# Four places of a hybrid decoder trunk in a new order: gate matmuls, retention scores, the end of the first RWKV half, and transposes of attention probabilities

## The chip, the cores and the metric

The kernel runs on one core of a Trainium2 chip. The metric is the time of one execution on the device in microseconds, lower is better. Three runs of the kernel before gave 884.91, 885.19 and 886.32 us, so its time is the median, 885.19 us.

## The reference

The program computes two decoder layers for 256 tokens of width 1024. Layer 0 mixes tokens with RWKV-7 (8 heads of 64) and with chunkwise retention (8 heads of 64) side by side; layer 1 mixes them with differential attention (8 heads, two softmaxes each). Each layer then attends to 256 memory tokens and runs an MLP of width 4096. The parts that the change touches are these:

```python
def rwkv7_time_mix(pa, mu, w0, w2, a0, a2, g2, k_k, k_a, r_k, ln_w, ln_b):
    ...
    w_log = -jax.nn.softplus(-(w0 + jnp.tanh(wd) @ w2)) - 0.5
    decay = jnp.exp(-jnp.exp(w_log.astype(jnp.float32)))
    a = jax.nn.sigmoid(a0 + ad @ a2)
    g = jax.nn.sigmoid(gd) @ g2
    ...
    y = wkv7_scan(r_h, hd(decay), k_h, v_h, -kk, kk * a_h)
    y = group_norm(y, ln_w, ln_b, A_GN_EPS)
    y = y + jnp.sum(r_h * k_h * r_k, axis=-1, keepdims=True) * v_h
    return y.reshape(bsz, s, A_WIDTH) * g

def retention(pb, ln_w):
    ...
    scores = jnp.einsum('bhncd,bhnmd->bhncm', qc, kc) * dmat[None, :, None]
    inner = jnp.einsum('bhncm,bhnme->bhnce', scores, vc)
    ...

def diff_attention(h, w_in, lq1, lk1, lq2, lk2, ln_w, w_out, rel_bias, lam_init):
    q, k, v = jnp.split(h @ w_in, 3, axis=-1)
    ...
    logits = jnp.einsum('bhcqd,bhckd->bhcqk', q_blk, k).astype(jnp.float32) * scale + bias[None, :, None]
    p = jax.nn.softmax(logits, axis=-1)
    attn = p[:, :, 0] - lam * p[:, :, 1]
    o = jnp.einsum('bhqk,bhke->bhqe', attn.astype(v.dtype), v)
    ...

def reference(x, mem, ...):
    for layer in range(DEPTH):
        ...
        h = h + mix
        h = h + memory_cross_attention(rms_norm(h, norm_cross_w[layer]), mem_n, ...)
        h = h + squared_relu_mlp(rms_norm(h, norm_mlp_w[layer]), mlp_w1[layer], mlp_w2[layer])
    return rms_norm(h, final_norm_w)
```

## The kernel before

**The weight stream.** All large products are f32 products made of three matmuls on rounded parts. A weight piece of 512 KB lands in `raw` (a DMA on SyncE's queue, four buffers). ScalarE writes its rounded high part `hi`, VectorE the rest `lo` (both line 129, three buffers each). TensorE multiplies high by high, low by high and high by low. These matmuls run through the whole program as a stream, piece after piece, 24 matmuls of 256 columns or 12 of 512 a piece. A second kind of matmul is plain f32 on small tiles; it shows in the trace as two records for each instruction.

**PSUM banks.** There are eight: four of the pool `acc`, two of `mm`, two of `tr` (functions `acc_t`, `mm_t`, `tr_t`). Whoever asks a pool for a tile gets its next bank in turn, and the first matmul into it waits until the last reader of that bank is done.

**What sets the order.** The framework's scheduler fixes the order of each engine's instructions when the program is built, by dependencies and by the order in which the code is written; on the chip each engine runs its list in that order.

**The gate stage (lines 425 to 434).** `psw` and `psa` are products of 64 rows each, one in the lower and one in the upper row half of the array (`w2a2[0:64]` and `w2a2[64:128]`), in two batches (`b0` of 0 and 2), with two `tr` banks a batch. ScalarE's sigmoids into `sg` (line 434) and `a` empty them. Then come products with the head pattern for `kk` (two columns each) and transposes of `v` (`tok_major`, line 500).

**Retention scores (lines 632 to 648).** `kTr` and `qTr` hold two heads in each 128 rows. For each `hq` and each row half `h2`, four matmuls fill one `mm` and one `tr` bank; VectorE multiplies by the mask (lines 646, 648) and ScalarE copies the rest (line 647). Beside this VectorE runs the triangular inverse of the RWKV part (lines 591, 593). `ret_T` (line 686) later transposes the retention output `xn`.

**The RWKV halves.** A loop over four groups `g` makes `LV`, `U` and states `S`. `outputs(0)` stands behind group 2, then `finish(0)` and `outputs(1)` behind the loop, then six `kv_chunk`s of memory keys and values. `outputs` ends in a group norm: `sm`, `yc`, `ysq`, `s2`, then `rs` on GpSimd (line 226), then `yc` times `rs` (line 748). `finish` transposes `yc` (line 757), applies weights on ScalarE (`ya`, line 759) and multiplies by the gate.

**Differential attention (lines 1077 to 1186).** For `c` of 0 to 3, `proj_cols` makes two heads of q and two of k from four weight pieces. `heads(hd)` makes a head's logits (`kTd`, `qTd`) and its softmaxes, subtracts them into `z` (line 1125), transposes `z` (line 1128) into a `tr` bank, and ScalarE copies that to `PTd` (line 1129). Heads of pair `c - 1` are written behind the projections of pair `c`. `v_proj` makes the values, `attend` multiplies `PTd` by `Vd`, `to_oT` transposes the result.

Of the kernel before, what the change touches and what calls it, by code (L numbers as in the profile page):

```python
# [8 lines left out]
F32 = mybir.dt.float32  # L9
F32R = mybir.dt.float32r  # L10
AF = mybir.ActivationFunctionType
# [26 lines left out]
def kernel(ctx: ExitStack, tc: tile.TileContext, ins: dict, out: bass.AP):  # L38
# [29 lines left out]
    def nm(s):  # L68
        cnt[0] += 1
        return f"{s}_{cnt[0]}"  # L70

    def acc_t():
        return ps_acc.tile([128, 512], F32, tag="acc", name=nm("acc"))

    def mm_t():
        return ps_mm.tile([128, 512], F32, tag="mm", name=nm("mm"))

    def tr_t():
        return ps_tr.tile([128, 512], F32, tag="tr", name=nm("tr"))
# [39 lines left out]
    def mm(o, lhsT, rhs, start, stop):  # L119

        ins = nc.tensor.matmul(o, lhsT=lhsT, rhs=rhs, start=start, stop=stop)  # L121
        key = o.tensor.name
        prev = last_in_bank.get(key)
        if prev is not None:
            behind(ins, prev, "one accumulation group per bank")
        last_in_bank[key] = ins
# [296 lines left out]
    a_ = t4(prep, "a")  # L423
    nc.scalar.activation(wa_[0:64, :], wa_[0:64, :], AF.Tanh)
    for b0 in (0, 2):
        psw = tr_t().rearrange("p (b t) -> p b t", b=2)
        psa = tr_t().rearrange("p (b t) -> p b t", b=2)
        for j in range(2):
            cs = slice((b0 + j) * 128, (b0 + j + 1) * 128)
            mm(psw[:, j, :], lhsT=w2a2[0:64, cs], rhs=wa_[0:64, :], start=True, stop=True)  # L430
            mm(psa[:, j, :], lhsT=w2a2[64:128, cs], rhs=wa_[64:128, :], start=True, stop=True)
        for j in range(2):
            b = b0 + j
            nc.scalar.activation(sg[:, b, :], psw[:, j, :], AF.Sigmoid, bias=prm[:, R_W0 + b:R_W0 + b + 1])
            nc.scalar.activation(a_[:, b, :], psa[:, j, :], AF.Sigmoid, bias=prm[:, R_A0 + b:R_A0 + b + 1])
# [193 lines left out]

    PT0 = []  # L630
    cmb = cmask.unsqueeze(1).broadcast_to([128, 2, 128])
    for hq in range(2):
        p0 = rp.tile([128, 4, 256], F32, tag=f"qk{hq}", name=nm("PT0"))
        p1 = PT1[hq]
        PT0.append(p0)
        for h2 in range(2):
            pr = slice(h2 * 64, h2 * 64 + 64)
            ps = mm_t().rearrange("p (h c) -> p h c", h=2)
            ps1 = tr_t()[:, :256].rearrange("p (h c) -> p h c", h=2)
            for i in range(2):  # L640
                hp = 2 * hq + i
                mm(ps[:, i, :], lhsT=kTr[pr, hp, 0:128], rhs=qTr[pr, hp, :], start=True, stop=True)
                mm(ps1[:, i, :], lhsT=kTr[pr, hp, 128:256], rhs=qTr[pr, hp, 128:256], start=True, stop=True)
            d0 = p0.rearrange("p (i h) c -> p h i c", i=2)[:, h2]
            d1 = p1.rearrange("p (i h) c -> p h i c", i=2)[:, h2]
            nc.vector.tensor_tensor(d0[:, :, 0:128], ps[:, :, 0:128], cmb, op=ALU.mult)
            nc.scalar.activation(d0[:, :, 128:256], ps[:, :, 128:256], AF.Copy)
            nc.vector.tensor_tensor(d1, ps1, cmb, op=ALU.mult)

    def g_evac(ps, t):  # L650
        nc.scalar.activation(gR[:, t, :], ps, AF.Sigmoid)
# [164 lines left out]
        if g == 2:  # L816
            outputs(0)

    finish(0)
    outputs(1)  # L820


# [1 line left out]
    V0 = xpool.tile([128, 2, D], F32, tag="xAl", name="V0")  # L824
    for i in range(6):
        kv_chunk(0, i, KT0, V0)
    KT1 = [kv1pool.tile([128, 8, 256], F32R, tag="KT1", name="KT1h")]
    V1 = kv1pool.tile([128, 2, D], F32, tag="V1", name="V1")
    kv1_left = [4, 5, 0, 1, 2, 3]
# [247 lines left out]
    def diff(before, after):  # L1077
# [15 lines left out]
        r1 = dp.tile([128, 2, 8], F32, tag="r1", name="r1")  # L1093
        r1q = dp.tile([128, 2, 8], F32, tag="r1q", name="r1q")

        def heads(hd):
            zt = [dp.tile([128, 2, 128 * (t + 1)], F32, tag=f"z{t}", name=nm("z"), bufs=2) for t in range(2)]

            ps = [acc_t() for _ in range(2)]
            for t in range(2):  # L1100
# [10 lines left out]
            for t in range(2):  # L1111
# [11 lines left out]
                cf = small.tile([128, 1], F32, tag="cf", name=nm("cf"))  # L1123
                nc.vector.tensor_scalar(cf, sm[:, 0:1], rc[:, 1:2], nlam, op0=ALU.mult, op1=ALU.mult)
                nc.vector.scalar_tensor_tensor(z3[:, 0, :], z3[:, 1, :], cf, z3[:, 0, :], op0=ALU.mult, op1=ALU.add)
                pt = tr_t()
                for k in range(t + 1):
                    nc.tensor.transpose(pt[:, k * 128:(k + 1) * 128], z3[:, 0, k * 128:(k + 1) * 128], ident)  # L1128
# [2 lines left out]
        for c in range(4):  # L1131
            proj_cols(I["w_dqk"], 2 * c, xT, lambda ps, c=c: nc.scalar.activation(qT[:, 2 * c:2 * c + 2, :], ps, AF.Copy), c == 0)
            proj_cols(I["w_dqk"], 8 + 2 * c, xT, lambda ps, c=c: nc.scalar.activation(kT[:, 2 * c:2 * c + 2, :], ps, AF.Copy))
            if c > 0:
                heads(2 * c - 2)
                heads(2 * c - 1)
        heads(6)
        heads(7)
        nc.vector.tensor_tensor(r1q, r1, r1, op=ALU.mult)
        oT = next_xT()  # L1140
        onorm = {}

# [4 lines left out]
        def attend(hq, t, po):  # L1147
# [8 lines left out]
            nc.scalar.activation(sq, o3, AF.Square)  # L1156
            s2 = small.tile([128, 4], F32, tag="s24", name=nm("s2"))
            nc.vector.tensor_reduce(s2, sq, axis=AX.X, op=ALU.add)
            nc.vector.tensor_tensor(s2, s2, r1q[:, t, 4 * hq:4 * hq + 4], op=ALU.mult)
            rs = rstd_of(s2, 128, 4, EPS)  # L1160
            nc.vector.tensor_tensor(rs, rs, r1[:, t, 4 * hq:4 * hq + 4], op=ALU.mult)
# [9 lines left out]
                         oT[1][:, 4 * hq:4 * hq + 4, t * 128:(t + 1) * 128], ps, wdif)  # L1171

        v_proj(0)
        for t in range(2):
            attend(0, t, acc_t())
        v_proj(1)
        for t in range(2):
            to_oT(0, t)
# [144 lines left out]
```

## Time and profile before

| what | value |
|---|---|
| median of three runs | 885.19 us |
| the profiled execution | 886.23 us |
| span of its trace | 884.5 us |
| TensorE busy | 864.1 us (98%) |
| VectorE busy | 590.8 us (67%) |
| ScalarE busy | 455.3 us (51%) |
| share of TensorE in the chain that ended last | 88% |

The profiled execution is 1.04 us above the median; 1.7 us of it lie outside the span. TensorE is the bound nearly everywhere, so a stage's time is that of TensorE's list plus TensorE's idle time, and the places to look at are its idle gaps, its slow records and the switches out of the stream.

### The profile page before, as it was taken

Reading aid. Unit: us, or ns where it says so; the run is one execution under the profiler, and the core shown is the slowest. Engines: PE = TensorE matmul, PEld = TensorE weight load, DVE = VectorE, ACT = ScalarE, POOL = GpSimd, SP = SyncE. Lnnn points to the kernel's source line nnn. Section 1 sums busy time; section 2 is a strip of 40 time slices with the busy share of each in tenths; the row PEclk is TensorE's granted clock in tenths of the full one; section 3 lists DMA queues with packets and bytes.
Section 4 is the critical chain, followed back from the end, with each engine's and each line's share of the span. In section 5 each row is a group of like instructions: output and inputs, shape, how many; then the busy total and the mean of one; then the engine's idle time right before and its main releaser. Section 6 shows DMA issues by size and latency. Waiting matters only on the chain.

```text
span 884.5 us, 14111 instructions
## 1 busy us (share of the span) xinstructions
PE 864.1 (98%) x5546; PEld 746.8 (84%) x5546; DVE 590.8 (67%) x932; ACT 455.3 (51%) x730; POOL 30.3 (3%) x51
## 2 busy tenths in 40 slices
PE   7999999999999999999999999999999999999996
PEld 5988889878889888888888899878998888888885
DVE  5668898564586576666666666786776776666665
ACT  5765444244475455444444455575654554444443
POOL 2000001010000000000000000001000000000001
PEclk7999999999999999999999999999999999999999
DMA  8654444125664647556566655534552465555561
GB/s 314 233 160 120 118 137 139 50 81 185 189 218 165 207 145 240 190 190 190 188 190 191 187 178 167 143 120 140 180 173 103 148 204 186 192 192 186 193 188 63
DMA packets 47078, 149.98 MB, mean 170 GB/s; under 512 B 4731, under 2 KB 4900, under 8 KB 46884
## 3 DMA queue, kind: packets, MB, share of 16 engines
q1 hardware_dynamic: 45456, 142.73, 50.0%
q10 hardware_dynamic: 1108, 3.72, 1.3%
q0 software_dynamic: 448, 2.63, 1.0%
q8 instruction: 43, 0.70, 0.3%
q14 instruction: 23, 0.19, 0.1%
HBM read 148.01 MB, written 2.63 MB: 170 GB/s over the span
## 4 chain that ended last, share of the span: by engine, by line
PE 88%; DVE 5%; issue 3%; ACT 2%; POOL 1%; DMA 1%; POOLq 0%; SPq 0%; DVEq 0%; ACTq 0%
PE acc L121 36%; PE mm L121 36%; PE tr L121 13%; DVE lo L129 1%; ACT hi L129 1%; PE tr L254 1%; POOL rs L226 1%; DMA h<-in_x_dram 1%; PE tr L1128 1%; PE tr L975 1%; DVE z L1109 0%; PE acc L254 0%; DVE xn L268 0%; PE tr L500 0%; POOL xn L1206 0%
## 5 line engine op out<-in xcount | busy, mean ns | idle before, releaser
L129 DVE TENSOR_TENSOR lo<-raw,hi 128x1024 fp32r<-128x1024 f32 x262 | 320.2, 1224 | 220.2 <-ACT hi L129 218.0
L129 ACT ACTIVATE hi<-raw 128x1024 fp32r<-128x1024 f32 x262 | 277.6, 1060 | 328.5 <-PE mm L121 119.6
L121 PE MATMUL mm<-xhl,hi 128*128 128x256 f32 (+1 forms) x784 | 188.0, 319 | 1.0 <-ACT xhl L129 0.7
L121 PEld LDWEIGHTS mm<-xhl,hi 128*128 128x128 f32 x784 | 129.7, 189 | 11.8 <-ACT xhl L129 1.7
L121 PE MATMUL mm<-xhl,lo 128*128 128x256 f32 x512 | 138.2, 282 | 0.0
L121 PE MATMUL acc<-hi,hl 128*128 128x512 f32 x256 | 100.2, 392 | 0.0
L121 PE MATMUL acc<-hi,hh 128*128 128x512 f32 x256 | 100.2, 391 | 0.0
L121 PE MATMUL acc<-lo,hh 128*128 128x512 f32 x256 | 99.7, 390 | 0.0
L121 PEld LDWEIGHTS mm<-xhl,lo 128*128 128x128 f32 x512 | 96.7, 189 | 2.5
L121 PE MATMUL tr<-xhl,hi 128*128 128x512 f32 x256 | 92.8, 396 | 0.0
L121 PE MATMUL acc<-hi,xhl 128*128 128x512 f32 x256 | 81.9, 396 | 0.0
L121 PE MATMUL tr<-xhl,lo 128*128 128x256 f32 x256 | 66.8, 281 | 0.0
L121 PEld LDWEIGHTS acc<-hi,hl 128*128 128x128 f32 x256 | 48.1, 188 | 11.2 <-DVE hl L129 0.9
L121 PEld LDWEIGHTS acc<-lo,hh 128*128 128x128 f32 x256 | 48.1, 188 | 10.4
L121 PEld LDWEIGHTS acc<-hi,xhl 128*128 128x128 f32 x256 | 47.8, 188 | 9.7
L121 PEld LDWEIGHTS acc<-hi,hh 128*128 128x128 f32 x256 | 48.1, 188 | 8.7
L121 PEld LDWEIGHTS tr<-xhl,hi 128*128 128x128 f32 x256 | 48.2, 188 | 8.4
L121 PEld LDWEIGHTS tr<-xhl,lo 128*128 128x128 f32 x256 | 48.3, 189 | 2.9
L121 PE MATMUL acc<-lo,xhl 128*128 128x512 f32 x128 | 50.4, 394 | 0.0
L121 PE MATMUL mm<-meml,hi 128*128 128x256 f32 x128 | 37.2, 291 | 0.0
L121 PE MATMUL mm<-memh,hi 128*128 128x256 f32 x128 | 37.1, 290 | 0.0
L121 PE MATMUL mm<-memh,lo 128*128 128x256 f32 x128 | 36.6, 286 | 0.0
(316 smaller groups left out, 1354.5 us busy)
## 6 DMA issues: line engine op xcount, KB each, us to landing
raw<-in_w_dram SPq DMA_DIRECT2D x64, 512.0 KB, 4.3
raw<-in_mlp_w_dram SPq DMA_DIRECT2D x64, 512.0 KB, 4.3
raw<-in_hyb_w_in_dram SPq DMA_DIRECT2D x16, 512.0 KB, 3.8
raw<-in_w_k_dram SPq DMA_DIRECT2D x16, 512.0 KB, 3.6
raw<-in_xattn_w_kv_dram SPq DMA_DIRECT2D x16, 512.0 KB, 3.7
raw<-in_w_q_dram SPq DMA_DIRECT2D x16, 512.0 KB, 4.5
raw<-in_xattn_w_o_dram SPq DMA_DIRECT2D x16, 512.0 KB, 3.5
raw<-in_w_dqk_dram SPq DMA_DIRECT2D x16, 512.0 KB, 3.4
```

Source lines behind the costliest of these rows:

```text
L121: ins = nc.tensor.matmul(o, lhsT=lhsT, rhs=rhs, start=start, stop=stop)
L129: return nc.scalar.activation(hi, src, AF.Copy), nc.vector.tensor_tensor(lo, src, r32(hi), op=ALU.subtract)
L226: nc.gpsimd.tensor_tensor(rs, ms, mhalf[:, :k], op=ALU.pow)
L254: nc.tensor.transpose(ps[:, k4, :], x[:, kt * 128:(kt + 1) * 128], ident)
L975: nc.tensor.transpose(pt[:, j, m, :], P[:, j, m * 128:(m + 1) * 128], ident)
L1128: nc.tensor.transpose(pt[:, k * 128:(k + 1) * 128], z3[:, 0, k * 128:(k + 1) * 128], ident)
```

## The change

Four edits, none of which alters what is computed.

- Gate stage: `psw` and `psa` come from pool `acc`, not `tr`.
- Retention scores: the two row halves are written in turn, matmul by matmul. `ps` comes from `mm` for `hq` 0 and from `acc` for `hq` 1, and `ps1` is two `tr` banks that both `hq` share.
- `outputs(1)` follows the loop at once; `finish(0)` is written behind the memory chunk `i == 3`.
- `heads` stops at `z`. A new function `turn_heads` makes the transposes and copies, and is called one projection pair later. `z` has three buffers, `heads(7)` stands behind `v_proj(0)`, and `r1q` is made in `attend`, four columns at a time.

```diff
     for b0 in (0, 2):
-        psw = tr_t().rearrange("p (b t) -> p b t", b=2)
-        psa = tr_t().rearrange("p (b t) -> p b t", b=2)
+        psw = acc_t().rearrange("p (b t) -> p b t", b=2)
+        psa = acc_t().rearrange("p (b t) -> p b t", b=2)
...
+    ps1 = [tr_t().rearrange("p (q h c) -> p q h c", q=2, h=2) for _ in range(2)]
     for hq in range(2):
...
+        ps = [(mm_t, acc_t)[hq]().rearrange("p (h c) -> p h c", h=2) for _ in range(2)]
+
+        for i in range(2):
+            hp = 2 * hq + i
+            for h2 in range(2):
+                pr = slice(h2 * 64, h2 * 64 + 64)
+                mm(ps[h2][:, i, :], lhsT=kTr[pr, hp, 0:128], rhs=qTr[pr, hp, :], start=True, stop=True)
+            for h2 in range(2):
+                pr = slice(h2 * 64, h2 * 64 + 64)
+                mm(ps1[h2][:, hq, i, :], lhsT=kTr[pr, hp, 128:256], rhs=qTr[pr, hp, 128:256], start=True, stop=True)
         for h2 in range(2):
-            pr = slice(h2 * 64, h2 * 64 + 64)
-            ps = mm_t().rearrange("p (h c) -> p h c", h=2)
-            ps1 = tr_t()[:, :256].rearrange("p (h c) -> p h c", h=2)
-            for i in range(2):
-                hp = 2 * hq + i
-                mm(ps[:, i, :], lhsT=kTr[pr, hp, 0:128], rhs=qTr[pr, hp, :], start=True, stop=True)
-                mm(ps1[:, i, :], lhsT=kTr[pr, hp, 128:256], rhs=qTr[pr, hp, 128:256], start=True, stop=True)
...
-    finish(0)
     outputs(1)
...
         kv_chunk(0, i, KT0, V0)
+        if i == 3:
+            finish(0)
...
+        zs = {}
+
         def heads(hd):
-            zt = [dp.tile([128, 2, 128 * (t + 1)], F32, tag=f"z{t}", name=nm("z"), bufs=2) for t in range(2)]
+            zt = [dp.tile([128, 2, 128 * (t + 1)], F32, tag=f"z{t}", name=nm("z"), bufs=3) for t in range(2)]
+            zs[hd] = zt
...
+
+        def turn_heads(hd):
+            for t in range(2):
+                n = 128 * (t + 1)
+                z3 = zs[hd][t]
                 pt = tr_t()
...
+            if c > 1:
+                turn_heads(2 * c - 4)
+                turn_heads(2 * c - 3)
             if c > 0:
                 heads(2 * c - 2)
                 heads(2 * c - 1)
         heads(6)
-        heads(7)
-        nc.vector.tensor_tensor(r1q, r1, r1, op=ALU.mult)
...
         v_proj(0)
+        turn_heads(4)
+        turn_heads(5)
+        heads(7)
         for t in range(2):
             attend(0, t, acc_t())
+        turn_heads(6)
+        turn_heads(7)
         v_proj(1)
```

The diff does not tell where the scheduler puts the moved work. Three places follow, each first as the kernel before has it and then as the changed one has it. A name is a buffer with its number, behind the arrow are the two operands, and x4 is four rows in a run. The order of SyncE's DMAs and of GpSimd is the same in both.

TensorE in the gate stage, before (`tr_738` and `tr_739` are the second batch, `acc_866` the stream):

```order
L121 MATMUL acc_866<-hi_869,xl_124 128x512
L121 MATMUL tr_738<-wa,w2a_195 128x256 x2
L121 MATMUL tr_739<-wa,w2a_195 128x256 x2
L121 MATMUL acc_866<-hi_869,xh_123 128x512
L121 MATMUL tr_769<-prm,kk_89_760 128x2 x8
L121 MATMUL acc_866<-lo_870,xh_123 128x512
L121 MATMUL acc_866<-hi_869,xl_124 128x512
L121 MATMUL acc_867<-hi_869,xh_123 128x512
L500 MATMUL tr_802<-prm,v_198 128x128 x4
L500 MATMUL tr_808<-prm,v_198 128x128 x4
```

and in the changed kernel:

```order
L121 MATMUL acc_738<-wa,w2a_195 128x256
L121 MATMUL acc_739<-wa,w2a_195 128x256
L121 MATMUL acc_738<-wa,w2a_195 128x256
L121 MATMUL acc_739<-wa,w2a_195 128x256
L121 MATMUL tr_769<-prm,kk_89_760 128x2 x8
L500 MATMUL tr_802<-prm,v_198 128x128 x4
L500 MATMUL tr_808<-prm,v_198 128x128 x4
L121 MATMUL acc_866<-hi_869,xh_123 128x512
```

The second batch now alternates its two banks, and gate, `kk` and `v` work stand in one row ahead of the stream's piece, which they cut three times before.

VectorE at the end of the first half, before (`lo_2230` and `lo_2248` belong to memory key pieces, the rest to `outputs(0)` and the group loop):

```order
L795 COPY U<-acc_1840 64x256
L129 TENSOR_TENSOR lo_2230<-raw_2228,hi_2229 128x1024
L740 TENSOR_SCALAR sm_1814<-sm_1814 128x8
L742 TENSOR_TENSOR yc_1817<-Y_1800,sm_1814 128x512
L746 TENSOR_REDUCE s_261_1821<-ysq_1819 128x8
L231 TENSOR_SCALAR ms_1823<-s_261_1821 128x8
L748 TENSOR_TENSOR yc_1817<-yc_1817,rs_1825 128x512
L129 TENSOR_TENSOR lo_2248<-raw_2246,hi_2247 128x1024
```

and in the changed kernel (four lines further down in the file):

```order
L799 COPY U<-acc_1838 64x256
L744 TENSOR_SCALAR sm_1812<-sm_1812 128x8
L746 TENSOR_TENSOR yc_1815<-Y_1798,sm_1812 128x512
L750 TENSOR_REDUCE s_259_1819<-ysq_1817 128x8
L129 TENSOR_TENSOR lo_2228<-raw_2226,hi_2227 128x1024
L231 TENSOR_SCALAR ms_1821<-s_259_1819 128x8
L740 TENSOR_TENSOR Y_1883<-tr_1885,Y_1883 128x4x64
L752 TENSOR_TENSOR yc_1815<-yc_1815,rs_1823 128x512
```

The `lo` of the next piece moved from ahead of `sm` and `yc` to a place between the sum of squares and `ms`; on ScalarE its `hi` now stands ahead of `ysq`, and on TensorE the transposes of line 757 stand ahead of the last matmul of one piece, where they stood behind three of the next.

TensorE in differential attention at the pair `c` of 2, before (inside the stream, where a first transpose stood):

```order
L121 MATMUL mm_5506<-xhl_5054,hi_5538 128x256
L1128 MATMUL tr_5447<-prm,z_5424 128x128
L121 MATMUL mm_5506<-xhl_5054,hi_5538 128x256
L121 MATMUL mm_5506<-xhl_5054,lo_5539 128x256
L121 MATMUL mm_5506<-xhl_5054,hi_5538 128x256 x2
```

and in the changed kernel (behind the pair's last piece; line 1141 is the transpose in `turn_heads`):

```order
L121 MATMUL mm_5552<-xhl_5052,lo_5585 128x256
L1141 MATMUL tr_5614<-prm,z_5422 128x128
L1141 MATMUL tr_5617<-prm,z_5423 128x128 x2
L121 MATMUL acc_5630<-kTd,qTd 128x128
L121 MATMUL acc_5631<-kTd,qTd 128x128
L121 MATMUL acc_5630<-kTd,qTd 128x256
L121 MATMUL acc_5631<-kTd,qTd 128x256
L1141 MATMUL tr_5621<-prm,z_5456 128x128
L121 MATMUL acc_5664<-kTd,qTd 128x128
L1141 MATMUL tr_5624<-prm,z_5457 128x128 x2
```

The four transposes of a pair stood at four places of the two streams; they now stand among the logits of the next pair, and four of them share two `tr` banks in a short stretch.

## Rows read from the trace of the kernel before

**Rows 1.** Busy times (page, part 1), chain that ended last (part 4)
```profile
PE 864.1 (98%) x5546; PEld 746.8 (84%) x5546; DVE 590.8 (67%) x932; ACT 455.3 (51%) x730; POOL 30.3 (3%) x51
...
PE 88%; DVE 5%; issue 3%; ACT 2%; POOL 1%; DMA 1%; POOLq 0%; SPq 0%; DVEq 0%; ACTq 0%
```

**Rows 2.** TensorE timeline, gate stage (start, duration, instruction, idle before and its releaser)
```profile
59.53 1.14 PE L121 MATMUL tr<-wa,w2a 64*128 64x256 f32 x8
60.59 0.50 PE L121 MATMUL acc<-hi,xh 128*128 128x512 f32 x1
60.93 0.39 PE L121 MATMUL acc<-lo,xh 128*128 128x512 f32 x1
61.16 0.40 PE L121 MATMUL acc<-hi,xl 128*128 128x512 f32 x1
61.76 1.86 PE L121 MATMUL tr<-wa,w2a 64*128 64x256 f32 x8 [0.21 <-ACT sg L434]
...
63.89 1.88 PE L121 MATMUL tr<-prm,kk 128*128 128x2 f32 x16
...
66.51 1.91 PE L500 MATMUL tr<-prm,v 128*128 128x128 f32 x8
...
70.05 0.39 PE L121 MATMUL acc<-hi,xh 128*128 128x512 f32 x1
```

**Rows 3.** Windows (length, busy per engine, granted clock, DMA share and rate)
```profile
66.30:69.60 3.30, 3.30 (x14) 2.81 (x13) 2.13 (x6) 0.89 (x1) 0.00 (x0) 0.50 0.00 0
127.50:131.00 3.50, 3.50 (x34) 3.50 (x33) 3.36 (x9) 2.25 (x4) 0.00 (x0) 1.00 0.54 165
543.25:603.77 60.52, 58.97 (x387) 49.98 (x385) 49.75 (x138) 38.50 (x105) 2.03 (x2) 1.00 0.42 128
```

**Rows 4.** Timeline of TensorE, both blocks of retention scores
```profile
110.37 0.70 PE L121 MATMUL mm<-qkT,qkT 64*128 64x256 f32 x2
...
112.63 0.51 PE L121 MATMUL acc<-hi,xh 128*128 128x512 f32 x1
...
114.47 0.70 PE L121 MATMUL mm<-qkT,qkT 64*128 64x256 f32 x2 [0.86 <-ACT PT L647]
...
116.73 0.51 PE L121 MATMUL acc<-hi,xh 128*128 128x512 f32 x1
```

**Rows 5.** Timeline of VectorE, its waits from 100 to 140 us
```profile
100.21 1.45 DVE L570 TENSOR_TENSOR SCb<-tr,prm 128x512 f32<-128x512 f32 x2 [0.51 <-PE tr L121]
...
115.86 0.42 DVE L646 TENSOR_TENSOR PT<-mm,prm 128x256 f32<-128x256 f32 x1 [0.16 <-PE mm L121]
...
133.44 0.69 DVE L673 TENSOR_REDUCE s<-xn 128x8 f32<-128x512 f32 x1 [0.68 <-ACT xn L671]
...
136.17 0.17 DVE L676 TENSOR_TENSOR rs<-rs,prm 128x8 f32<-128x8 f32 x1 [1.54 <-POOL rs L226]
```

**Rows 6.** Timeline of TensorE at ret_T, line 686
```profile
139.15 0.66 PE L686 MATMUL tr<-prm,xn 128*128 128x128 f32 x4 [0.21 <-DVE xn L679]
```

**Rows 7.** Timeline of VectorE, group norm of the first half
```profile
180.57 1.23 DVE L129 TENSOR_TENSOR lo<-raw,hi 128x1024 fp32r<-128x1024 f32 x1
...
186.00 0.69 DVE L748 TENSOR_TENSOR yc<-yc,rs 128x512 f32<-128x512 f32 x1 [1.75 <-POOL rs L226]
```

**Rows 8.** Timeline of TensorE at finish(0) and behind it
```profile
186.75 0.66 PE L757 MATMUL tr<-prm,yc 128*128 128x128 f32 x4 [1.26 <-DVE yc L748]
...
189.16 0.68 PE L121 MATMUL tr<-S,AR 64*64 64x64 f32 x16
```

**Rows 9.** Waits from 543 to 604 us: in total, times, longest
```profile
PE tr L1128 <- DVE z L1125: 0.9, 2, 0.4
```

**Rows 10.** Timeline of TensorE at heads(6)
```profile
574.76 1.16 PE L121 MATMUL acc<-kTd,qTd 64*128 64x128 f32 x8 [0.58 <-DVE z L1109]
```

**Rows 11.** Timeline of ScalarE ahead of it
```profile
571.74 1.06 ACT L129 ACTIVATE hi<-raw 128x1024 fp32r<-128x1024 f32 x1 [1.95 <-issue]
572.70 0.58 ACT L1133 ACTIVATE kTd<-mm 128x512 f32<-128x512 f32 x1
```

More of the change, by code (lines that the diff above doesn't have):

```diff
@@ L635 @@
         PT0.append(p0)
-        for h2 in range(2):
-            pr = slice(h2 * 64, h2 * 64 + 64)
-            ps = mm_t().rearrange("p (h c) -> p h c", h=2)
-            ps1 = tr_t()[:, :256].rearrange("p (h c) -> p h c", h=2)
-            for i in range(2):
-                hp = 2 * hq + i
-                mm(ps[:, i, :], lhsT=kTr[pr, hp, 0:128], rhs=qTr[pr, hp, :], start=True, stop=True)
-                mm(ps1[:, i, :], lhsT=kTr[pr, hp, 128:256], rhs=qTr[pr, hp, 128:256], start=True, stop=True)
+        ps = [(mm_t, acc_t)[hq]().rearrange("p (h c) -> p h c", h=2) for _ in range(2)]
[7 more added lines that the diff above has]
+                mm(ps1[h2][:, hq, i, :], lhsT=kTr[pr, hp, 128:256], rhs=qTr[pr, hp, 128:256], start=True, stop=True)
+        for h2 in range(2):
             d0 = p0.rearrange("p (i h) c -> p h i c", i=2)[:, h2]
             d1 = p1.rearrange("p (i h) c -> p h i c", i=2)[:, h2]
-            nc.vector.tensor_tensor(d0[:, :, 0:128], ps[:, :, 0:128], cmb, op=ALU.mult)
-            nc.scalar.activation(d0[:, :, 128:256], ps[:, :, 128:256], AF.Copy)
-            nc.vector.tensor_tensor(d1, ps1, cmb, op=ALU.mult)
+            nc.vector.tensor_tensor(d0[:, :, 0:128], ps[h2][:, :, 0:128], cmb, op=ALU.mult)
+            nc.scalar.activation(d0[:, :, 128:256], ps[h2][:, :, 128:256], AF.Copy)
+            nc.vector.tensor_tensor(d1, ps1[h2][:, hq], cmb, op=ALU.mult)
     def g_evac(ps, t):
@@ L1158, in attend @@
             nc.vector.tensor_reduce(s2, sq, axis=AX.X, op=ALU.add)
+            r1h = r1[:, t, 4 * hq:4 * hq + 4]
+            nc.vector.tensor_tensor(r1q[:, t, 4 * hq:4 * hq + 4], r1h, r1h, op=ALU.mult)
             nc.vector.tensor_tensor(s2, s2, r1q[:, t, 4 * hq:4 * hq + 4], op=ALU.mult)
```

## The prediction, made before the changed kernel ran

> **What bounds the kernel now.** I read the page first. TensorE is busy 98% of the span and 88% of the chain that ended last is its own [rows 1], so an edit pays only where it shortens TensorE's own list or its idle time. Next I read TensorE's timeline at each of the four edited places and noted three things: idle gaps with their releaser, records that run longer than their like, and the price of leaving the weight stream. Then I followed the engines that TensorE waits for, since a stage that gets shorter may only meet a later wait. The price of a switch comes from the gate stage: the first stream matmul behind small work lasts 0.34 us from start to start (60.59 to 60.93), the next 0.23 [rows 2], so coming back costs 0.11. From 61.16 to 61.76 are 0.60 us; less 0.23 of matmul and 0.21 of idle that leaves 0.16 for going out [rows 2]. A trip out of the stream is thus 0.27 at a wait, and I take 0.2 where a bank stands ready.
>
> **Gate stage.** Two batches of eight records stand there now. The first, whose row halves alternate, lasts 1.06 us to the next stream matmul (59.53 to 60.59). The second, whose halves do not alternate, lasts 1.86, behind a wait of 0.21 for ScalarE to empty a `tr` bank [rows 2]. With four `acc` banks both batches run as the first does: 1.06 and at most 1.06 in place of 1.06 and 1.86, which saves 0.8, and the wait of 0.21 goes. Between `kk`, `v` and the gate work three trips out of the stream fall away, 3 x 0.27 = 0.8. Against that, the transposes of `v` now come right behind `kk`, where by my walk VectorE has `v` and the sum of `kk` ready only 0.3 us after TensorE arrives. Net 0.8 + 0.2 + 0.8 - 0.3 = 1.5 us.
>
> The second term is the clock. From 66.3 to 69.6 us the granted clock is 0.50, that is 1.2 and not 2.4 GHz [rows 3]; the transposes of `v` and five stream matmuls run in it. What came before was the serial second batch, one stream matmul, the 16 `kk` records of two columns each and three stream matmuls [rows 2]. Half speed over 3.3 to 3.4 us costs 1.7 us. In the changed order the dense alternating batches stand directly ahead of `kk`, and the stream follows without a break. Small f32 work alone does not lower the clock: from 127.5 to 131 us TensorE ran 34 records with 64 columns each and kept 1.00 [rows 3]. I take it that the fall does not come, a saving of 1.7; the other end is 0, or a loss of as much if a second fall follows. So this edit gives 3.2 us at TensorE, and I carry on 3.0, since VectorE's work up to 104 us (it waits for TensorE, 0.51 us at 100.21 [rows 5]) follows with little to spare.
>
> The Trainium skill, "TensorE: Matmul & The Clock Gate", Part 4, says that transposes on TensorE do not count as busy work for the clock in the way that matmuls do. The changed order puts eight transposes right behind the 16 two-column records, so by that rule the stretch of weak work gets no stronger where I count on it, and the fall would stay: 881.4 us, rival 1 below. The trace here shows transposes only inside the fall, not ahead of it, so it neither agrees nor disagrees.
>
> **Retention scores.** Two blocks last 2.26 us each (110.37 to 112.63, 114.47 to 116.73), with 0.86 of idle ahead of the second, where a bank waits for ScalarE's copy [rows 4]. With halves alternating, a pair of 64-row records runs at once, as in the first gate batch. I estimate one block at 2.6 us: the eight score matmuls of each old block, 64-row throughout, at half of their serial time. Saved: 4.5 + 0.9 + 0.3 for one trip - 2.6 = 3.1 us at TensorE.
>
> But VectorE works here almost without a break. Between 104 us and `ret_T` it waits three times: 0.16 for a score matmul, 0.68 for ScalarE and 1.54 for GpSimd's `rs` [rows 5]. The last follows VectorE's own result and does not shrink. TensorE already waits for VectorE at `ret_T`, 0.21 us [rows 6]. If TensorE comes 3.1 earlier, VectorE can come only 0.16 + 0.68 = 0.84 earlier, and some 2.3 us come back as idle time at line 686. I carry 0.8; the ends are 0.5 and 3.1.
>
> **The end of the first half.** TensorE waits 1.26 us at line 757 for `yc` [rows 8], which itself waits 1.75 for GpSimd [rows 7]. A `lo` of 1.23 us stands ahead of `sm` and `yc` [rows 7]. The changed lists move that `lo` behind the sum of squares but ahead of `ms`, and put a `hi` (1.06 us, as the one of rows 11) ahead of `ysq` on ScalarE, so one delay replaces another, and my walk has `yc` ready only 0.35 us earlier. TensorE arrives with four stream matmuls fewer done (4 x 0.23 = 0.9) and the 32 small `S,AR` records already behind it. Those cost two trips of 0.61 us each (189.16 [rows 8] and one like it) and about 0.45 inside the group loop. At the end of the stretch: 0.35 earlier at line 757, less 0.9 of stream left over, plus 1.2 of `S,AR` no longer there: 0.7 us saved. The wait at line 757 grows to about 1.6 in this account. Ends: 0 (the `hi` is late) and 1.5.
>
> **Differential attention.** From 543.25 to 603.77 us TensorE is idle 60.52 - 58.97 = 1.55 us [rows 3]: 0.9 in two waits of a transpose for `z` [rows 9], 0.58 at `heads(6)` [rows 10]. All of this can go, and of some 20 trips out of the stream 14, at 0.2 each: 2.8. Gross 4.3 us. What comes in place: four transposes of a pair share two `tr` banks, so the third waits for ScalarE's copy of the first, and ScalarE has a `hi` (1.06) and the copy of `kTd` (0.58) queued at that moment [rows 11]. TensorE does the next logits meanwhile, which covers half of it; I get 0.8 us at `c` of 2, 0.8 at 3, 0.75 behind `v_proj(0)` (where the copy to `Vd` also stands ahead) and 1.0 inside `v_proj(1)`, where `heads(7)` is fresh. 4.3 - 3.35 = 1.0 us saved. Ends: 2.6 saved (the copies slip ahead of the `hi`), 1.5 lost.
>
> **Sum.** 3.0 + 0.8 + 0.7 + 1.0 = 5.5 us off the profiled execution of 886.23, hence 880.7; the median of three stands 1.04 lower, so 885.19 - 5.5 = 879.7 us. Between the four places the stream is TensorE's own, so nothing there takes the gain back.
>
> **Rivals.** (1) The clock still falls once in the gate stage. 1.7 us are not saved: 881.4 us. For it: the 16 two-column records and the transposes now stand in a row. Against it: the dense batches ahead. By the skill's rule above this is what happens. Chance 0.18. (2) VectorE has more room than its timeline shows, since its score products now come together and one ScalarE wait ends earlier; then the whole 3.1 of the scores arrives: 879.7 - 2.3 = 877.4 us. Against it: the 0.21 at line 686. Chance 0.10. (3) The gate gain does not pass VectorE's list between 70 and 104 us and is given back there: 879.7 + 3.0 = 882.7. Chance 0.10. (4) Nothing is left: the clock falls, the first half's end gives nothing and the bunched transposes lose 1.5: 885.19 - 1.3 - 0.8 + 1.5 = 884.6. Chance 0.10. (5) Slower, by one mechanism: in the bunches every third and fourth transpose waits out a `hi` and a `kTd` copy uncovered, 1.64 us [rows 11]. Four bunches with two such waits are 13.1 us, 9.8 more than I count, so 879.7 + 9.8 = 889.5. It decides against the change once these waits cost 5.5 + 3.35 = 8.9 us in all, 1.1 each. Against it: ScalarE is busy only 38.5 of 60.5 us there [rows 3]. Chance 0.06. That the edit on the scores does nothing, because halves do not overlap, I rule out by the two gate batches, 1.06 against 1.86 [rows 2].
>
> **How the numbers follow.** The forecast keeps 0.46. The range goes from 876.5, below rival 2 with a little of the better ends, to 884.0; it leaves out rivals 4 and 5 and some edge. A measurement of this kernel can tell about 0.2%, that is 1.8 us. Faster than 883.4: the forecast, rivals 1 and 2 and nearly all of rival 3, less the bad ends, 0.80. Slower than 887.0: rival 5 and a little, 0.07. Between: 0.13.
>
> **What would show it.** Gate stage: the next piece's first matmul near 67 us, not 70.05, with the granted clock at 1.00 throughout; 68.5 with half clock means rival 1. Scores: one block of 2.6 us with no idle time in it, and then 2 us or more of idle at `ret_T` for `xn`; without that idle, rival 2. First half: line 757 still waiting for `yc`, 1.3 to 1.9 us. Differential attention: unbroken streams, and at the bunches transposes that wait for `PTd`; over 8.9 us of such waits means rival 5. The prediction is wrong if TensorE shows a new gap above 1 us at another place than these.

## The result

The changed kernel takes 879.58 us (median of four runs, 879.29 to 880.91), the kernel before 885.39 us in the same job. The ratio is 0.9936, with a 95% interval of 0.9924 to 0.9949: 5.8 us faster, forecast 5.5. Nine executions of the changed kernel over two jobs have the median 880.00 us. In the second job the medians are 881.31 and 885.47 us, only 4.2 apart. The total came out as forecast; three of the four terms that make it up did not, and part of the agreement is luck.

The page of the changed kernel (the lines that answer to [rows 1]):

```profile
PE 856.3 (98%) x5546; PEld 741.5 (84%) x5546; DVE 589.3 (67%) x935; ACT 456.4 (52%) x730; POOL 32.1 (4%) x51
...
PE 90%; DVE 4%; issue 2%; ACT 2%; POOL 1%; DMA 1%; SPq 0%; POOLq 0%; ACTq 0%; DVEq 0%
```

TensorE's busy time fell by 7.8 us, its share of the chain rose to 90%. But the profiled execution, 879.56 us, is 6.7 below the profiled one of before, more than the medians are apart, and the difference starts ahead of the first edit. Both kernels begin with a stretch at half clock (columns: length, busy time of five engines, granted clock, DMA share, GB/s). Changed kernel:

```profile
9.60:12.80 3.20, 3.20 (x16) 2.81 (x16) 3.02 (x5) 2.10 (x4) 0.24 (x1) 0.52 1.03 422
13.00:18.00 5.00, 3.63 (x28) 3.44 (x29) 4.71 (x7) 3.04 (x5) 1.43 (x1) 0.98 1.03 341
```

Kernel before:

```profile
8.30:18.40 10.10, 7.71 (x33) 7.05 (x34) 9.00 (x14) 5.19 (x9) 2.04 (x3) 0.50 1.03 374
```

The granted clock is 0.5 for some 3 us in the one and for 10 us in the other, with the same instructions. In all traces of this case it is at 0.5 there for 3.4, 6.8 or 10.2 us together, whatever the kernel, and the 13th `lo` of line 129 then starts at 46.8 to 47.6, 47.9 to 48.8 or 48.5 to 48.9 us. So I compare stages only from that `lo` on (48.50 us before, 46.77 after: 1.73 us of mere luck). The table gives how much earlier than in the kernel before four later `lo` stand, counted from there: number 25 (behind the gate stage), 37 (behind `ret_T`), 73 (behind the first half) and 181 (behind differential attention). Negative is earlier, in us.

| kernel | 25 | 37 | 73 | 181 | median of its executions |
|---|---|---|---|---|---|
| changed kernel | -3.29 | -3.13 | -4.27 | -4.94 | 879.58 |
| after_again (the changed kernel once more) | -3.24 | -3.05 | -4.06 | -4.73 | 881.31 |
| gate_back | -0.07 | 0.07 | -1.05 | -1.67 | 884.20 |
| scores_back | -3.25 | -3.23 | -4.27 | -4.89 | 880.77 |
| finish_back | -3.28 | -1.54 | -1.39 | -2.00 | 884.58 |
| turn_back | -3.32 | -3.12 | -4.18 | -4.20 | 881.53 |
| reads_last | -3.31 | -4.26 | -5.30 | -5.95 | 879.56 |
| reads_last_short_inverse | -3.31 | -0.91 | -3.25 | -3.79 | 882.86 (one run) |
| finish_later | -3.30 | -1.57 | -4.15 | -4.85 | 880.12 |
| scores_back_finish_later | -3.30 | -3.29 | -5.68 | -6.32 | 879.05 |
| reads_last_finish_later | -3.31 | -2.71 | -5.31 | -5.84 | 879.32 |
| gate_serial | -2.96 | -2.82 | -3.85 | -4.39 | 881.75 (one run) |
| kk_twice | 1.82 | 3.51 | 2.47 | 1.85 | 888.21 (one run) |

By its first line the four edits give 3.29, -0.16, 1.14 and 0.67 us, 4.94 in all. The forecast had 3.0, 0.8, 0.7 and 1.0. Its second line, the same kernel traced again, differs by up to 0.21 us, so the table can tell no less than that. The measured 5.8 and 4.2 lie on either side of 4.94; the spread of the start, about 2 us, is enough for both.

### The profile page after: what moved, and what is told of

Its sections match the earlier page's. It is cut to its first block, busy times and chain, and to the rows that moved or that the text cites. A ratio compares the mean times of both kernels' runs of the same rounds, so it can differ in the third digit from the quotient of the medians.

```text
span 877.8 us, 14116 instructions
## 1 busy us (share of the span) xinstructions
PE 856.3 (98%) x5546; PEld 741.5 (84%) x5546; DVE 589.3 (67%) x935; ACT 456.4 (52%) x730; POOL 32.1 (4%) x51
## 4 chain that ended last, share of the span: by engine, by line
PE 90%; DVE 4%; issue 2%; ACT 2%; POOL 1%; DMA 1%; SPq 0%; POOLq 0%; ACTq 0%; DVEq 0%
PE acc L121 37%; PE mm L121 37%; PE tr L121 13%; DVE lo L129 1%; ACT hi L129 1%; POOL rs L226 1%; PE tr L254 1%; DMA h<-in_x_dram 1%; PE tr L980 1%; PE acc L254 1%; DVE xn L268 0%; PE tr L500 0%; POOL xn L1227 0%; PE tr L1141 0%; PE tr L552 0%
```

## Experiments: each edit undone

Four kernels each undo one edit and keep the other three.

**The gate stage.** gate_back takes the tiles from `tr` again:

```diff
-        psw = acc_t().rearrange("p (b t) -> p b t", b=2)
-        psa = acc_t().rearrange("p (b t) -> p b t", b=2)
+        psw = tr_t().rearrange("p (b t) -> p b t", b=2)
+        psa = tr_t().rearrange("p (b t) -> p b t", b=2)
```

> The changed kernel with psw and psa in tr banks again; all else as changed. If the gate edit is worth what the trace of the changed kernel shows (3.3 us, half of it the clock), the time is 3.3 us above the changed kernel, near 883, and the granted clock falls to 0.5 for about 3.4 us near 66 us again. If the fall of the clock has nothing to do with the edit, the clock stays at 1.00 there and the time rises by only 1.5 to 1.6 us.

It measured 884.20 us (883.18 to 885.45), and the whole gain of 3.2 us behind the stage is gone. The medians are 4.6 us apart, the traces 3.3 at the last column; the executions spread by more than their difference. TensorE in the changed kernel (start, duration, instruction):

```profile
57.72 2.00 PE L121 MATMUL acc<-wa,w2a 64*128 64x256 f32 x16
59.65 1.95 PE L121 MATMUL tr<-prm,kk 128*128 128x2 f32 x16
61.45 1.08 PE L500 MATMUL tr<-prm,v 128*128 128x128 f32 x8
62.29 0.48 PE L121 MATMUL acc<-hi,xh 128*128 128x512 f32 x1
...
65.17 0.40 PE L121 MATMUL acc<-hi,xh 128*128 128x512 f32 x1
```

Sixteen gate records last 1.93 us to the first of `kk`, and no idle time is left, against [rows 2]. The next piece begins at 65.17, where it began at 70.05; without the 1.73 of the start that is 3.15 earlier. The clock there in the changed kernel:

```profile
59.00:63.00 4.00, 4.00 (x35) 3.55 (x32) 3.28 (x6) 4.00 (x12) 0.00 (x0) 1.00 0.69 236
63.00:66.27 3.27, 3.27 (x15) 2.63 (x15) 2.41 (x6) 3.24 (x4) 0.00 (x0) 1.00 0.05 18
66.27:69.70 3.43, 3.43 (x16) 2.74 (x16) 3.43 (x4) 2.82 (x4) 0.00 (x0) 1.00 0.11 15
```

and in gate_back, at the same stage:

```profile
64.90:68.10 3.20, 3.20 (x13) 2.78 (x12) 2.49 (x8) 1.06 (x1) 0.00 (x0) 0.51 0.00 0
```

The half-speed stretch of [rows 3] is gone with the edit and back without it. All eleven traces that have the edit and the `kk` records once lack it, both traces without the edit have it. Where two kernels do the same work up to number 37 and one of them has a fall of 3.4 us further on, that fall costs 1.55 to 1.59 us (finish_back and finish_later against the changed kernel, reads_last_finish_later against reads_last). So by estimate about half of the 3.29 us is the clock and the other half the shorter list; no run separates the two.

**The retention scores.** scores_back has the old loop over `h2`, row half by row half, with its own banks each:

```diff
-            for h2 in range(2):
-                pr = slice(h2 * 64, h2 * 64 + 64)
-                mm(ps[h2][:, i, :], lhsT=kTr[pr, hp, 0:128], rhs=qTr[pr, hp, :], start=True, stop=True)
...
+            ps = mm_t().rearrange("p (h c) -> p h c", h=2)
+            ps1 = tr_t()[:, :256].rearrange("p (h c) -> p h c", h=2)
```

> The changed kernel with the retention scores as before (row half by row half). By the prediction's term the time is 0.8 us above the changed kernel. By the theory from its trace (the shared tr banks make TensorE wait 2.0 us for VectorE inside the block, so that the edit gives nothing) it is within 0.2 us of it, and the transposes at ret_T stand at the same place, 0.0 to 0.3 us earlier.

880.77 us (880.70 to 881.26); its profiled run had 6.8 us at half clock at the start, the changed kernel's 3.4. Counted behind that, everything from 37 on stands within 0.1 us of the changed kernel. The edit is worth nothing that these traces can tell (in whole times scores_back lies between the changed kernel's two medians, 879.58 and 881.31). TensorE in the changed kernel's block shows why:

```profile
105.38 0.70 PE L121 MATMUL mm<-qkT,qkT 64*128 64x256 f32 x4
...
106.79 0.60 PE L121 MATMUL acc<-qkT,qkT 64*128 64x256 f32 x4
109.39 0.49 PE L121 MATMUL tr<-qkT,qkT 64*128 64x128 f32 x2 [2.00 <-DVE PT L652]
...
111.12 0.51 PE L121 MATMUL acc<-hi,xh 128*128 128x512 f32 x1
```

The block lasts 5.74 us, 105.38 to 111.12, and 2.00 of them are idle: the second `hq` writes the other half of the two `tr` banks that the first filled, and waits until VectorE has read them. VectorE, in the same place:

```profile
107.45 1.22 DVE L129 TENSOR_TENSOR lo<-raw,hi 128x1024 fp32r<-128x1024 f32 x1
...
108.92 0.41 DVE L652 TENSOR_TENSOR PT<-tr,prm 128x256 f32<-128x256 f32 x1
...
109.58 0.41 DVE L652 TENSOR_TENSOR PT<-tr,prm 128x256 f32<-128x256 f32 x1
...
128.52 0.69 DVE L677 TENSOR_REDUCE s<-xn 128x8 f32<-128x512 f32 x1 [1.00 <-ACT xn L675]
```

It has a `lo` (107.45) ahead of these reads; the first `tr` read starts at 108.92 and the second at 109.58. The 0.86 us of idle in [rows 4] became 2.00. Behind the wait the two halves also no longer alternate cleanly, since each `tr` bank comes free on its own. VectorE then waits 1.00 us for ScalarE's `xn` at 128.52 (it was 0.68 in [rows 5]), and `ret_T` waits for VectorE in turn, 0.38 us against 0.21 in [rows 6]. From the start of the block to `ret_T` are 28.95 us, against 28.78 from the first old block [rows 4, 6]:

```profile
134.33 0.63 PE L690 MATMUL tr<-prm,xn 128*128 128x128 f32 x4 [0.38 <-DVE xn L683]
```

**The first half's end.** finish_back:

```diff
+    finish(0)
     outputs(1)
...
-        if i == 3:
-            finish(0)
```

> The changed kernel with finish(0) ahead of outputs(1) again. By the trace, 1.1 us above the changed kernel, all of it between 170 and 195 us, with two S,AR trips out of the stream again; by the prediction's term 0.7. The wait of line 757's transposes for yc stays within 0.1 of 1.28 us either way.

The time is 884.58 us, and its executions lie between 882.16 and 886.96, far more apart than one edit explains. Between `lo` 37 and 73 the changed kernel gains 1.14 us; finish_back loses 0.15. So by the traces the edit's own worth is near 1.1 to 1.3. But finish_back stands 1.6 us behind the changed kernel already at 37, ahead of anything that it changes:

```profile
112.10:115.30 3.20, 3.20 (x9) 2.42 (x9) 2.89 (x12) 0.29 (x1) 0.00 (x0) 0.50 0.02 5
```

The granted clock is 0.50 right behind the score block with its 2 us of idle. The other kernels with that wait go on below. Edit and fall make 2.9 us, while the medians are 5.0 apart: half of the executions, 885.40 to 886.96, have a mean granted clock of 0.988 to 0.990 against 0.994 in the traced one, and where they lost it no trace shows. What the edit is worth in whole times stays open by that. The edit itself in the changed kernel, VectorE first, then ScalarE, then TensorE:

```profile
176.85 0.69 DVE L750 TENSOR_REDUCE s<-ysq 128x8 f32<-128x512 f32 x1 [0.82 <-ACT ysq L748]
177.58 1.22 DVE L129 TENSOR_TENSOR lo<-raw,hi 128x1024 fp32r<-128x1024 f32 x1
178.72 0.16 DVE L231 TENSOR_SCALAR ms<-s 128x8 f32<-128x8 f32 x1
...
180.63 0.69 DVE L752 TENSOR_TENSOR yc<-yc,rs 128x512 f32<-128x512 f32 x1 [1.29 <-POOL rs L226]
```

```profile
175.24 1.06 ACT L129 ACTIVATE hi<-raw 128x1024 fp32r<-128x1024 f32 x1 [0.25 <-PE mm L121]
176.20 0.61 ACT L748 ACTIVATE ysq<-yc 128x512 f32<-128x512 f32 x1
```

```profile
181.38 0.66 PE L761 MATMUL tr<-prm,yc 128*128 128x128 f32 x4 [1.28 <-DVE yc L752]
```

`yc` starts its last step at 180.63 and not at 186.00 [rows 7]; of these 5.37 us 1.73 are the start's and 3.13 came from the stages ahead, so 0.5 are its own; a `lo` (177.58) still stands in its chain and a `hi` (175.24) ahead of `ysq`. TensorE's wait is 1.28 us, as long as in [rows 8]; the rest of the gain is the two `S,AR` trips that are no longer there, less four stream matmuls left to do (0.9). The kernel before, around the trip at 189.16 in [rows 8]:

```profile
188.83 0.40 PE L121 MATMUL mm<-hi,memh 128*128 128x512 f32 x1
...
190.10 0.39 PE L121 MATMUL mm<-hi,meml 128*128 128x512 f32 x1
```

From 188.83 to 190.10 are 1.27 us, less 0.46 for two stream matmuls: the trip costs 0.81, and so does the next. 0.5 + 1.6 - 0.9 = 1.2, against 1.14 measured.

**The transposes.** turn_back has them in `heads` again:

```diff
-            if c > 1:
-                turn_heads(2 * c - 4)
-                turn_heads(2 * c - 3)
...
+        heads(7)
+        nc.vector.tensor_tensor(r1q, r1, r1, op=ALU.mult)
```

> The changed kernel with the transposes of the attention probabilities in heads again, z in two buffers, heads(7) ahead of v_proj(0). By the trace 0.65 us above the changed kernel, all of it between 540 and 610 us; by the prediction's term 1.0. A single measurement of the whole time can hardly tell these two apart; the markers in the trace can.

881.53 us, 880.80 to 885.07 (three of eight executions are above 882.9, at a lower mean granted clock than the others and without a trace); in the trace the 0.7 us between 161 and 181 are not gained, and nothing else differs by over 0.1. In the changed kernel, TensorE's waits from 536 to 598 us (in total, times, longest):

```profile
PE tr L1141 <- ACT PTd L1142: 1.0, 2, 0.5
...
PE acc L121 <- ACT Vd L1159: 0.5, 1, 0.5
PE tr L1141 <- DVE z L1133: 0.5, 1, 0.5
```

Two us of new waits against the 1.5 us of old ones in [rows 9, 10]. The first bunch shows how they arise, TensorE and then ScalarE:

```profile
548.75 0.49 PE L1141 MATMUL tr<-prm,z 128*128 128x128 f32 x3
549.17 0.93 PE L121 MATMUL acc<-kTd,qTd 64*128 64x128 f32 x8
550.65 0.33 PE L1141 MATMUL tr<-prm,z 128*128 128x128 f32 x1 [0.55 <-ACT PTd L1142]
```

```profile
548.89 1.06 ACT L129 ACTIVATE hi<-raw 128x1024 fp32r<-128x1024 f32 x1 [1.79 <-PE mm L121]
549.85 0.58 ACT L1146 ACTIVATE kTd<-mm 128x512 f32<-128x512 f32 x1
550.33 0.97 ACT L1142 ACTIVATE PTd<-tr 128x128 f32<-128x128 f32 x3
```

The next transpose (550.65) waits for the copy of the first to `PTd`, and ScalarE has a `hi` and the copy of `kTd` ahead of them, as forecast; the logits between cover most of it. TensorE leaves the stream 21 times in this stage in turn_back and in the kernel before, 7 times in the changed kernel, so 14 trips are gone as forecast. The price of a trip was the term that was too large. From turn_back, in the stream of 512 columns:

```profile
574.30 0.39 PE L121 MATMUL mm<-hi,xhl 128*128 128x512 f32 x1
574.54 0.38 PE L1133 MATMUL tr<-prm,z 128*128 128x128 f32 x2
574.67 0.48 PE L121 MATMUL mm<-hi,xhl 128*128 128x512 f32 x1
574.99 0.39 PE L121 MATMUL mm<-lo,xhl 128*128 128x512 f32 x1
```

From 574.30 to 574.99 are 0.69 us for two stream matmuls (0.23 each) and two transpose records of 0.11: the trip costs nothing there.

## Experiments: what the waits do to the clock, and what would be better

**Does the changed kernel spread too?** after_again is the changed kernel unaltered.

> The changed kernel itself, to see how its executions spread. In the variant with finish(0) put back, the granted clock fell to 0.5 for 3.4 us right behind the 2.0 us in which TensorE waits inside the score block, and its executions lay between 882.2 and 887.0. If that wait is what lets the clock fall, some executions of the changed kernel do the same and lie 1.5 to 4 us above its 879.3; if it belongs to the variant alone, all of them lie between 879 and 881.

881.71, 881.31, 881.64, 879.59 and 880.00 us. Three lie 2.0 us or more above 879.3; the profiled one of them, 881.71, had a start stretch of 10.2 us and no fall at the score block. No execution of the changed kernel lies in finish_back's 882 to 887. The fall behind the score block is in the traces of finish_back, finish_later and kk_twice (below), which all have the wait, not in those of gate_back, gate_serial, turn_back and the two of the changed kernel, which have it too (1.99 to 2.01 us), and not in scores_back, which has not. The wait can let the clock fall and need not; what decides is open.

**All score matmuls ahead of the reads.** reads_last only moves the reads into a loop of their own:

```diff
+    pss = []
     ps1 = [tr_t().rearrange("p (q h c) -> p q h c", q=2, h=2) for _ in range(2)]
...
+        pss.append(ps)
+
+    for hq in range(2):
+        p0, p1, ps = PT0[hq], PT1[hq], pss[hq]
         for h2 in range(2):
```

> The changed kernel, but all 16 score matmuls are written ahead of the reads of their banks, so that the second hq no longer waits for VectorE to read the shared tr banks. Theory (VectorE sets the pace from 104 us to ret_T): the score block takes 2.6 to 2.9 us without idle time instead of 5.7; ret_T's transposes stand only 0.9 us earlier than in the changed kernel, with 2 us or more of idle ahead of them, waiting for xn; whole time 0.9 below the changed kernel's fastest. Rival (VectorE has room): 3 us below, and no idle at ret_T. Third: a clock that falls behind the idle time at ret_T instead takes the gain back in some executions.

879.56 us (879.48 to 880.24). The block:

```profile
106.72 0.70 PE L121 MATMUL mm<-qkT,qkT 64*128 64x256 f32 x4
...
109.54 0.50 PE L121 MATMUL acc<-hi,xh 128*128 128x512 f32 x1
```

and `ret_T`:

```profile
134.54 0.63 PE L695 MATMUL tr<-prm,xn 128*128 128x128 f32 x4 [2.18 <-DVE xn L688]
```

The block is 2.82 us long without idle time, and 2.18 us of idle stand at `ret_T` instead, for the same `xn` as in [rows 6]. It is what the prediction described for the changed kernel itself. Number 37 stands 1.1 us earlier than in the changed kernel, 181 stands 1.0 earlier. The rival with 3 us falls. The whole time did not come out 0.9 below the changed kernel's fastest (879.48 against 879.29); the traced execution had 6.8 us at half clock at its start.

**VectorE relieved.** reads_last_short_inverse runs 24 of the 31 row steps:

```diff
-        for k in range(31, 0, -1):
+        for k in [*range(31, 24, -1), *range(17, 0, -1)]:
```

> reads_last with seven of the 31 row steps of the triangular inverse (k of 24 to 18, two VectorE instructions each, some 3.5 to 3.9 us) left out; the inverse and all that hangs on it are not computed in full. If VectorE's list is what holds ret_T back, TensorE's idle 2.18 us ahead of it goes to under 0.3 and ret_T stands about 2 us earlier from the score block than in reads_last. If the wait is for something else (ScalarE's copies, GpSimd's rs), ret_T stays within 0.5 us of its place.

One run, 882.86 us. `ret_T` stands 0.9 us nearer to the 13th `lo` than in reads_last, where 2 were expected and 0.5 was the other theory's bound. It tells neither apart. TensorE's idle time ahead of `ret_T`, expected to go under 0.3 us, grew to 2.87, since TensorE's own list is in another order there too, and behind it the clock fell to 0.50 for 3.4 us, which is part of the longer time. The scheduler filled the room: it moved later row steps ahead, so VectorE reached the sum of squares for `xn` only 0.2 us earlier, and what came earlier was due to a `lo` that now stands behind `xn`. That VectorE's list alone sets the pace is supported by reads_last, not shown by this run.

**finish(0) one chunk later.** finish_later changes one number:

```diff
-        if i == 3:
+        if i == 4:
             finish(0)
```

> The changed kernel with finish(0) behind memory chunk 4 in place of 3, so that a whole piece of stream stands between yc's group norm and its transposes. The wait of 1.28 us for yc at line 757 goes, nothing else waits longer: 1.2 to 1.3 us earlier from 195 us on. Rival: ya and the gate product then come too late for what follows and the stream's own lo waits; then under 0.5.

880.12 us (879.22 to 880.76). Line 757's transposes (761 here) no longer wait:

```profile
190.68 0.60 PE L761 MATMUL tr<-prm,yc 128*128 128x128 f32 x4
```

From 37 to 73 it gains 2.58 us where the changed kernel gains 1.14, so 1.4 more. It lost as much before: its profiled run had the fall of the clock behind the score block (1.57 against 3.13 at number 37).

**Without the wait in the block.** scores_back_finish_later has the scores of before, `finish(0)` at `i == 4` and the other two edits.

> Scores as in the kernel before, finish(0) behind chunk 4, the rest as changed. If the wait in the score block is what lets the clock fall, this kernel has no such executions: all within 1 us of each other at about 879.5 (880.8 of the variant with the scores put back, less 1.25). If the spread comes from elsewhere, some lie 3 us or more above.

878.70, 879.14, 878.34, 879.88 and 879.05 us, median 879.05, ratio 0.9926 (0.9914 to 0.9939). No execution stands out; they spread by 1.5 us, more than the 1 us expected and less than 3. As none of the changed kernel's nine executions was as slow as finish_back's either, five do not show that the wait is the cause. In the same job the changed kernel had 881.31 (0.9945).

**Both gains.** reads_last_finish_later has the reads last and `finish(0)` at `i == 4`.

> Both gains in one kernel: score matmuls ahead of all reads, finish(0) behind chunk 4. 1.0 and 1.4 us below the changed kernel's trace, so near 877.5 to 878.3, with no clock fall in the score block; a fall behind the 2.2 us of idle at ret_T in some executions would be seen as a spread above 1.7 us.

Six executions fall into two groups: 877.09, 878.02 and 878.30, and 880.34, 880.48 and 880.79; the median is 879.32. The profiled one belongs to the second, and its clock falls behind the idle time at `ret_T`:

```profile
133.10:135.20 2.10, 0.00 (x0) 0.00 (x0) 2.10 (x5) 1.08 (x2) 1.08 (x1) 1.00 0.00 0
135.30:138.50 3.20, 3.20 (x16) 3.20 (x17) 3.20 (x10) 0.37 (x1) 0.00 (x0) 0.50 0.55 170
```

TensorE does nothing for 2.1 us, and then runs at 0.50. This kernel has the fastest single execution of all. Against the kernel before in the same job its median does not differ from that of scores_back_finish_later (0.9924 and 0.9926).

**What lets the clock fall in the gate stage.** kk_twice issues the two-column records of `kk` twice:

```diff
-    for hf in range(2):
+    for hf in (0, 1, 0, 1):
         for b in range(4):
```

> The changed kernel with the 16 two-column records of kk issued twice into the same bank, 1.7 to 1.8 us more of them in the row ahead of v's transposes. If it is a longer row of such weak records that lets the clock fall, the granted clock goes to 0.50 for 3.4 us in or behind the gate stage and the stage's end moves by 3.5 us; if the clock was kept by the dense batches ahead whatever follows, it stays at 1.00 and the end moves by 1.7 to 1.8.

One run, 888.21 us. The clock:

```profile
59.55:61.48 1.93, 1.93 (x18) 1.47 (x17) 0.80 (x1) 1.89 (x4) 0.00 (x0) 1.00 0.56 122
63.90:70.40 6.50, 6.50 (x26) 6.02 (x26) 3.37 (x7) 3.18 (x6) 0.00 (x0) 0.50 0.17 63
```

It falls inside the longer row of `kk`, and for 6.8 us rather than 3.4; the stage's end moves by 5.1 us, 1.6 more than the larger of the two expected, which is the second 3.4 us. So the dense batches ahead do not keep the clock whatever follows: with 16 records behind them it stayed at 1.00, with 32 it fell. Which part of the new order keeps it with 16, the denser second batch or the stream that no longer cuts the row three times, no run separates.

gate_serial writes each batch row half by row half:

```diff
-            mm(psw[:, j, :], lhsT=w2a2[0:64, cs], rhs=wa_[0:64, :], start=True, stop=True)
-            mm(psa[:, j, :], lhsT=w2a2[64:128, cs], rhs=wa_[64:128, :], start=True, stop=True)
...
+        for rows, to in ((slice(0, 64), psw), (slice(64, 128), psa)):
+            for j in range(2):
...
+                mm(to[:, j, :], lhsT=w2a2[rows, cs], rhs=wa_[rows, :], start=True, stop=True)
```

> The changed kernel with both batches written row half by row half (two matmuls on the lower rows, then two on the upper) in the same acc banks. If overlap needs matmuls that alternate one by one, the 16 records last 2.8 to 3.6 us in place of 1.95; the clock falls if half-filled rows count as weak work, since weak work then stands ahead of kk as it did in the kernel before, and the end moves by 1 to 1.7 us without a fall, 2.7 to 3.4 with one. If only the number of switches matters, the end stays within 0.3 us.

One run, 881.75 us, with 6.8 us at half clock at the start; the stage's end moves by 0.33 us.

```profile
59.40 2.10 PE L121 MATMUL acc<-wa,w2a 64*128 64x256 f32 x16
61.43 1.95 PE L121 MATMUL tr<-prm,kk 128*128 128x2 f32 x16
```

Sixteen records take 2.03 us, against 1.93 when they alternate. In gate_back the second batch alone takes 1.86 in that order:

```profile
60.75 1.86 PE L121 MATMUL tr<-wa,w2a 64*128 64x256 f32 x8 [0.21 <-ACT sg L434]
```

So the order of the halves is worth 0.1 us of the 0.33; further down the scheduler has TensorE's list in another order, and the rest was not traced to a cause. What made the second batch long was its banks, which ScalarE emptied one after the other. In the kernel before, ScalarE's two reads `a` of the second bank, and the weight load (PEld) of the first record of the upper half:

```profile
61.59 0.85 ACT L435 ACTIVATE a<-tr,prm 128x256 f32<-128x256 f32 x2
62.49 0.29 PEld L121 LDWEIGHTS tr<-wa,w2a 64*128 64x128 f32 x2
```

The reads end at 62.44 and the upper half starts 0.05 us later; the lower half, at 61.76, started 0.05 us behind the last `sg`. The order is not always free, though: in the old score block [rows 4] eight records of the lower half stand ahead of the first of the upper, which starts at 111.13, 0.76 us behind the lower one at 110.37, with no wait shown.

## The prediction, step by step

- **The gate stage, 3.0 forecast, 3.29 measured.** The size and the end of the half-speed stretch were right, and the next piece came where it was looked for (65.17, that is 66.9 with the 1.73 of the start; 67 forecast). Two reasons were not. The second batch was slow for its banks and not for its order (gate_serial). And the dense batches ahead do not by themselves keep the clock (kk_twice). Rival 1 had the fall stay, since two-column records and transposes stand in a row: here eight transposes ran right behind 16 such records at a granted clock of 1.00. The Trainium skill, "TensorE: Matmul & The Clock Gate", Part 4, says that transposes do not count as busy in the way that matmuls do. The fall that was read out of this did not come here, which neither bears the statement out nor refutes it. That `v` would come 0.3 us late was wrong too: there is no gap ahead of its transposes.
- **The scores, 0.8 forecast, -0.16 measured.** The step that failed is "I estimate one block at 2.6 us". It takes 2.82 where nothing waits (reads_last), but in the changed kernel it lasts 5.74: the two `hq` share `tr` banks, and I had overlooked that the second has to wait until the first is read. The following step, that TensorE meets VectorE's pace, was right in kind and, as reads_last bears out with 1.0 us gained for 0.8 forecast, in size: 2.3 us at line 686 forecast, 2.00 inside the block and 0.38 at `ret_T` measured, 2.18 at `ret_T` in reads_last. What to look for, "one block of 2.6 us with no idle time in it", did not hold: a new gap of 2.00 us stands where none was to be.
- **The first half, 0.7 forecast, 1.14 measured.** `yc` is ready 0.5 us earlier (0.35 forecast), and the wait is 1.28 (1.6 forecast); it stays within the stated ends. The trips of `S,AR` were under-sized: 0.61 counts neither the way out of the stream nor the way back, with which each costs 0.81.
- **Differential attention, 1.0 forecast, 0.67 measured.** Both sides were too large. New waits are 2.0 us and not 3.35. The 14 trips give by difference 0.67 + 2.0 - 1.5 = 1.2 us, 0.09 each, not 0.2: at the one place of the 512-column stream that is shown, the transposes cost their own records and no more. Rival 5, the uncovered copies, is far off.
- **The sum, 5.5 forecast, 4.94 in the trace and 5.8 between the medians.** The sum did not contain the spread of the start as a term, although the profile before showed 0.50 in its first 20 us; at about 2 us from end to end it is larger than three of the four terms. Rivals 2 to 4 did not come: there is no full 3.1 from the scores, and the gate gain passes VectorE's list whole (-3.29 at 25, -3.26 at the 29th `lo`).

## What to carry to other kernels

Before counting on a denser block of matmuls, follow each bank in it to its last reader: in this kernel two halves of one bank are one bank to the waits, and a block that no longer waits for one engine may wait for the next. An edit on an engine that is the bound may be worth little if another engine paces the same stretch: with all matmuls ahead of the reads, 2.9 us less of score block gave 1.0 us. When stages are worth 1 us each, compare them in traces from a common point behind the start, and judge a version by several executions.

## What the runs showed of the hardware

- The clock stood at 0.5 near the start for 3.4, 6.8 or 10.2 us in executions with the same instructions there. The work behind it then begins up to 2 us later, about as much as most executions of the kernel before spread in one job (20 of 23 from 884.61 to 886.45, the others up to 887.39).
- Some 2 to 3 us without a matmul in an otherwise full stretch can cost 1.55 to 1.59 us more: a granted clock of 0.50 for 3.4 us followed the idle time in some traces (finish_back, finish_later, kk_twice, reads_last_finish_later, reads_last_short_inverse) and not in others (the changed kernel's two, gate_back, gate_serial, turn_back, reads_last). What decides it these runs do not show.
- Matmuls on opposite row halves overlapped without alternating one by one where four records of a half stood in a row and their banks were ready (2.03 against 1.93 us for 16 records, though gate_serial's list has both matmuls of the lower half ahead of the upper half's). Where eight stood in a row, the other half began 0.76 us late, and two blocks of 2.26 us took 4.5 in place of 2.82.
